# Seeding PSUM from ScalarE, separate steps for the low weight parts, and two more pairs by seven products, in a one-core hybrid attention block

## The chip, the cores and the metric

The kernel runs on one core of a Trainium2 chip. The metric is the device time of one execution in microseconds (us), the median of three runs. The kernel before takes 421.79 us (runs: 422.27, 421.79, 421.65).

The names of the engines: PE is TensorE, which multiplies matrices (PEld: its weight loads), DVE is VectorE, ACT is ScalarE, POOL is GpSimd, SP issues transfers. Matrix products land in PSUM, eight banks of 128 x 512 fp32 each (here `ps0` to `ps7`). Everything else lives in SBUF.

## What is computed

One layer of a streaming encoder: 512 tokens, width 1024. One input projection feeds two attention branches; each result is gated, projected, and both are merged and projected once more.

```python
h = rmsnorm(x, norm_g[l])
(q_lat, c_kv, k_rope, z_a, q_b, k_b, v_b, z_b,
 q_idx, k_idx, w_idx, gate_a, gate_b) = jnp.split(h @ w_in[l], cuts, axis=-1)
...
y_a = mla_attention(q_nope, q_pe, k_nope, k_pe, v_a, pos) * silu(z_a)
# branch b: each query keeps the 128 best keys by an indexer score, logits get a bias by distance
y_b = dsa_attention(q_b, k_b, v_b, q_idx, k_idx, w_idx, rel_bias, pos, topk) * silu(z_b)
merged = sigmoid(gate_a) * (y_a @ w_o_a[l]) + sigmoid(gate_b) * (y_b @ w_o_b[l])
out = rmsnorm(x + merged @ w_out[l], final_g)
```

## The kernel before, in words

**Numbers in two parts.** Every fp32 operand of a large product is split into a high part (rounded by ACT, `act(hi, raw)`) and a low part (`lo = x - hi`, on DVE or POOL, `lo_part`). A product is three matmuls: high x high, high x low, low x high (`mm3`).

**Order.** The program is made by a planner (`Flow`). Each piece of work is a generator ("thread") with a priority; it asks for buffers, waits for conditions, and yields steps. The planner estimates when each step could start, takes the earliest one and emits it to its engine's queue. On the chip each engine works its queue strictly in that order, so PE's order is fixed when the program is built. Numbers at the end of the file (`SEED`, `PSCORE`, `QUEUE`, `SPARE` and others) set priorities, buffer limits and the order of the weight jobs.

**Jobs.** `QUEUE` lists the weight jobs. A lower-case name (`zb1`) is a plain job: `proj` multiplies one 128-column tile of weights with all 512 tokens, 8 x 3 = 24 matmuls of 128x512. Names in upper case come in pairs (`GB0 GB1`): `proj2` makes two tiles from seven half products instead of eight (Winograd's form of Strassen's method), each of 12 matmuls of 128x256. In `seven` the partial sums are put together: ACT copies a finished PSUM bank into an SBUF tile `s_pair`, and DVE adds PSUM banks to it.

**Heads of branch b.** For each of eight heads `dsa_base` adds the reversed bias row and the mask of kept keys on DVE into the tiles `s_p`, ahead of time. `dsa_head` then has PE make the logits of four query tiles (128, 256, 384 and 512 keys wide), two matmuls each, in any bank that is free. DVE adds `s_p` and takes the maximum (line 1946), ACT takes the exponential, PE turns the tiles (identity matmuls, line 477) and multiplies them with the values `vv`.

**End.** `s_ys` (gated attention results) go through 192 matmuls, `s_wo` through the last ones, and `finish` and `scale_out` normalise and store.

**What touches what.** `split_w`, `split_t` and their callers: low parts. `seven`: order of the products and partial sums. `dsa_base`, `dsa_head`: bias and mask. `Pool_.give`: which free bank is taken. `QUEUE`: `zb0` to `zb3`.

Of the kernel before, what the change touches and what calls it, by code (L numbers as in the profile page):

```python
# [16 lines left out]
ALU = mybir.AluOpType  # L17
# [29 lines left out]
class Buf:  # L47


    def __init__(self, tile, name):  # L50
        self.tile, self.name, self.w, self.r, self.written = tile, name, 0.0, 0.0, False
        self.by, self.reads, self.bank = None, {}, False
# [71 lines left out]
class Pool_:  # L124
# [163 lines left out]
SEED = 1  # L288
# [5 lines left out]
def tile_block(ctx: ExitStack, tc: tile.TileContext, a: dict, out: bass.AP, bias_dram: bass.AP):  # L294
# [32 lines left out]
    for b in PS.free:  # L327
        b.bank = True
# [125 lines left out]
    def mm(ps, pairs, start, stop, more=False):  # L454


        def emit():
            for i, (l, r) in enumerate(pairs):
                nc.tensor.matmul(ps.ap, l.ap, r.ap, start=start and i == 0, stop=stop and i == len(pairs) - 1, skip_group_check=more)  # L459
# [12 lines left out]
    def turn(parts):  # L472


        def emit():
            for d, s in parts:
                nc.tensor.transpose(d.ap, s.ap, ident.tile)  # L477
# [94 lines left out]
    def warm_up():  # L572

        ps = yield bank("pv")
        z = zero.tile.bitcast(BF16)
        for _ in range(NWARM):
            yield pe(0.43, [ps.all], [zero.all], lambda: nc.tensor.matmul(  # L577
                ps.tile.rearrange("p (a b) -> p a b", b=P), z, z.rearrange("p (a b) -> p a b", a=1).to_broadcast([P, NT, P]), start=True, stop=True))
        put(ps)
# [103 lines left out]
    def split_w(raw, w, dst, key, cls="w", cap=None, release=False, early=False, added=False, high=None):  # L683
# [6 lines left out]
        if added and not early:  # L690
            yield from lo_added(lo[:, :w], raw, hi[:, :w])
        else:
            step = lo_part(lo[:, :w], raw, hi[:, :w])
            yield soon(step) if early else step
        if release:
            put(raw.buf)
        dst[key] = (hi, lo)
# [209 lines left out]
    def scores(i):  # L907
        n = P * (i + 1)
        work = mask_in_order(i)
        for h in range(NH):  # L910
            yield Until(lambda: h in qs and ks)
            ps = yield bank("lg")
            yield pe(0.005 + n / 2400, [ps.all], [qs[h].all, ks[0].all], lambda: nc.tensor.matmul(  # L913
                ps.tile[:, :n], qs[h].tile[:96, TOK[i]], ks[0].tile[:96, :n], start=True, stop=True))
# [114 lines left out]
    def bias_table():  # L1029
# [16 lines left out]
        for tp, o, c0, c1 in ((toep, oh[0], 0, 320), (toep2, oh[1], 320, 640)):  # L1046
            ps = yield bank("pv")
            yield pe(0.148, [ps.all], [rbs.all, o.all], lambda: nc.tensor.matmul(
                ps.tile[:, :320], rbs.tile, o.tile[:, :320], start=True, stop=True))
# [30 lines left out]
    def splitter():  # L1080
        for job in jobs:
# [7 lines left out]
            for p, w in enumerate(job.widths):  # L1089
                o = sum(job.widths[:p])  # L1090
                yield from split_w(job.raw[:, o : o + w], w, job.parts, p, job.cls, job.cap, p == len(job.widths) - 1, high=job.high, added=w == S and job.src.tensor.name in ADDW and (p > 0 or len(job.widths) == 1))
# [73 lines left out]
    def proj2(first, second):  # L1165
# [7 lines left out]
        def split_t(n, x):  # L1173
# [4 lines left out]
            if n in ADDP:  # L1178
# [1348 lines left out]
```

## Time and profile before

| | |
|---|---|
| runs | 422.27, 421.79, 421.65 us, median 421.79 |
| profiled execution, span from first to last instruction | 420.8 us (the page gives no other time of that execution; 1.0 us under the median) |
| PE | 2414 matmuls in the record |
| last matmul of the program begins and ends in | the piece from 408.47 to 414.27 us |
| end of the last computing instruction | 417.21 us (ACT, from 416.49, 0.72 us) |

The profile is read in this order below: the page's head (busy shares), the waits of PE's weight loads, matmul counts in stretches of time, and then the groups of instructions that the change adds or removes. A matmul's row in the profile has a duration of several hundred ns because it covers the passage through the array; several are in flight at once, so the issue interval, and not that duration, is what a matmul costs.

### The profile page before, as it was taken

To read this page: it belongs to the slowest core of one execution; us is meant where nothing else is said; L and a number is where in the kernel's file an instruction comes from. 1 tells how busy PE (TensorE), PEld (TensorE's weight loads), DVE (VectorE), ACT (ScalarE), POOL (GpSimd) and SP (SyncE) were. 2 spreads that over 40 slices of the span, in tenths; PEclk is the share of its full clock that TensorE was granted. 3 is DMA by queue.
4 is the path that set the end of the run, shared out by engine and by line. 5 is a ranking of instruction groups with operands and counts; after the bars stand their busy time and mean duration, and the time that the engine had idled before them with its cause. 6 is when DMAs were issued, how large, how long until landed. Compare 5 with 4: busy or idle time off the path is not lost.

```text
span 420.8 us, 7354 instructions
## 1 busy us (share of the span) xinstructions
PE 412.9 (98%) x2414; PEld 367.8 (87%) x2414; DVE 387.0 (92%) x845; ACT 273.1 (65%) x612; POOL 98.2 (23%) x122
## 2 busy tenths in 40 slices
PE   9999999999999999999999999999999999999993
PEld 6999988898888888888999998899988888888883
DVE  4869899999999999999889999999999887999984
ACT  5786997476484778647745488496578834346634
POOL 1023766535546434102111010021000100000212
PEclk9999999999999999999999999999999999999997
DMA  8973435906546721351334626441684884738205
GB/s 256 394 286 118 140 106 151 251 26 170 152 99 165 213 72 58 119 138 50 95 107 151 170 95 178 136 125 29 175 275 138 288 291 136 242 104 254 113 2 199
DMA packets 30279, 65.90 MB, mean 157 GB/s; under 512 B 4649, under 2 KB 5689, under 8 KB 30241
## 3 DMA queue, kind: packets, MB, share of 16 engines
q1 hardware_dynamic: 29120, 63.82, 48.8%
q0 software_dynamic: 832, 1.22, 1.2%
q8 instruction: 19, 0.31, 0.3%
q10 hardware_dynamic: 288, 0.39, 0.3%
q14 instruction: 20, 0.16, 0.1%
HBM read 50.49 MB, written 4.21 MB: 130 GB/s over the span
## 4 chain that ended last, share of the span: by engine, by line
PE 84%; DVE 8%; ACT 3%; issue 1%; DMA 1%; POOL 1%; POOLq 0%; DVEq 0%; ACTq 0%
PE ps L459 75%; PE ps L477 4%; DVE s_w L382 2%; DMA raw<-w_o 1%; PE ps L1830 1%; PE ps L1831 1%; PE ps L1829 1%; PE ps L577 1%; PE ps L913 1%; ACT s_p L360 1%; DVE s_p L1946 1%; DVE s_y L382 1%; ACT s_w L351 1%; DVE s_p L382 1%; POOL raw L384 1%
## 5 line engine op out<-in xcount | busy, mean ns | idle before, releaser
L459 PE MATMUL ps<-s_h,s_w 128*128 128x512 f32 (+1 forms) x696 | 152.0, 362 | 0.0
L459 PEld LDWEIGHTS ps<-s_h,s_w 128*128 128x128 f32 x696 | 114.6, 189 | 16.1
L351 ACT CAST s_w<-raw 128x512 fp32r<-128x512 f32 (+3 forms) x130 | 74.6, 594 | 24.0 <-DMA raw<-w_o 8.1
L382 DVE TENSOR_TENSOR s_w<-raw,s_w 128x512 fp32r<-128x512 f32 (+2 forms) x93 | 60.1, 663 | 4.1 <-ACT s_w L351 2.6
L384 POOL TENSOR_TENSOR s_w<-raw,s_w 128x512 fp32r<-128x512 f32 (+2 forms) x37 | 44.2, 1197 | 78.9 <-ACT s_w L351 56.0
L459 PE MATMUL ps<-s_ys,s_w 128*128 128x512 f32 x192 | 44.0, 390 | 0.1
L459 PEld LDWEIGHTS ps<-s_ys,s_w 128*128 128x128 f32 x192 | 36.0, 188 | 7.9 <-DVE s_ys L394 0.4
L459 PE MATMUL ps<-s_hs,s_w 128*128 128x256 f32 x288 | 40.2, 285 | 0.1
L459 PEld LDWEIGHTS ps<-s_hs,s_w 128*128 128x128 f32 x288 | 36.8, 191 | 0.5 <-DVE s_pair L382 0.3
L459 PE MATMUL ps<-s_wo,s_mg 128*128 128x512 f32 (+1 forms) x156 | 33.0, 373 | 0.0
L459 PE MATMUL ps<-s_w,s_xg 128*128 128x328 f32 (+1 forms) x192 | 32.8, 324 | 0.1
L360 ACT ACTIVATE s_p<-s_p,sm 128x512 f32<-128x512 f32 (+3 forms) x56 | 30.5, 563 | 3.3 <-DVE sm L1946 2.4
L459 PEld LDWEIGHTS ps<-s_wo,s_mg 128*128 128x128 f32 x156 | 27.6, 188 | 5.2
L459 PEld LDWEIGHTS ps<-s_w,s_xg 128*128 128x128 f32 x192 | 31.4, 188 | 0.6 <-ACT s_rbc L351 0.5
L939 DVE MATCH_REPLACE8 mask<-sm,mask 128x256 f32<-128x256 f32 (+2 forms) x48 | 25.8, 541 | 0.0
L938 DVE MAX8 sm<-mask 128x8 f32<-128x256 f32 (+2 forms) x48 | 25.1, 547 | 0.1
L360 ACT ACTIVATE s_p<-ps,sm 128x128 f32<-128x128 f32 (+3 forms) x32 | 16.7, 527 | 9.7 <-DVE sm L1814 9.4
L477 PE MATMUL ps<-ident,s_p 128*128 128x128 f32 x160 | 22.8, 273 | 0.0
L459 PE MATMUL ps<-s_lat,s_w 128*128 128x512 f32 x78 | 21.0, 397 | 0.0
L477 PEld LDWEIGHTS ps<-ident,s_p 128*128 128x128 f32 x160 | 18.7, 140 | 2.4
L382 DVE TENSOR_TENSOR s_ph<-ps,s_ph 128x512 fp32r<-128x512 f32 (+1 forms) x32 | 18.5, 614 | 0.6 <-ACT s_ph L351 0.6
L382 DVE TENSOR_TENSOR s_pair<-ps,s_pair 128x256 f32<-128x256 f32 (+1 forms) x35 | 15.9, 455 | 2.0 <-PE ps L459 1.9
(211 smaller groups left out, 767.9 us busy)
## 6 DMA issues: line engine op xcount, KB each, us to landing
raw<-w_out SPq DMA_DIRECT2D x18, 512.0 KB, 4.7
s_op<-s_op SPq DMA_DIRECT2D x36, 128.0 KB, 3.0
raw<-w_ga SPq DMA_DIRECT2D x8, 512.0 KB, 4.2
raw<-w_gb SPq DMA_DIRECT2D x8, 512.0 KB, 3.9
raw<-w_o SPq DMA_DIRECT2D x16, 256.0 KB, 3.3
s_x<-xT SPq DMA_DIRECT2D x8, 256.0 KB, 4.9
s_xn<-x SPq DMA_DIRECT2D x8, 256.0 KB, 6.3
raw<-w_za SPq DMA_DIRECT2D x4, 512.0 KB, 4.8
```

What stands on the lines that cost most here:

```text
L351: nc.scalar.copy(dst.ap, src.ap)
L360: nc.scalar.activation(dst.ap, src.ap, func, **kw)
L382: opts.append(("DVE", 0.07 + 0.00104 * x.n, lambda: nc.vector.tensor_tensor(dst.ap, x.ap, y.ap, op=op)))
L384: opts.append(("POOL", 0.15 + 0.0021 * x.n, lambda: nc.gpsimd.tensor_tensor(dst.ap, x.ap, y.ap, op=op)))
L459: nc.tensor.matmul(ps.ap, l.ap, r.ap, start=start and i == 0, stop=stop and i == len(pairs) - 1, skip_group_check=more)
L477: nc.tensor.transpose(d.ap, s.ap, ident.tile)
L577: yield pe(0.43, [ps.all], [zero.all], lambda: nc.tensor.matmul(ps.tile.rearrange("p (a b) -> p a b", b=P), z, z.rearrange("p (a b) -> p a ...
L913: yield pe(0.005 + n / 2400, [ps.all], [qs[h].all, ks[0].all], lambda: nc.tensor.matmul(ps.tile[:, :n], qs[h].tile[:96, TOK[i]], ks[0].til ...
L938: yield Step([("DVE", t, lambda: nc.vector.max(m8.tile, work.ap))], [m8], [mask[i]])
L939: yield Step([("DVE", t + 0.068, lambda: nc.vector.match_replace(work.ap, m8.tile, work.ap, MARK))], [mask[i]], [m8])
L1829: nc.tensor.matmul(o, q0[0:100], k0[0:100], start=True, stop=False)
L1830: nc.tensor.matmul(o, q0[0:96], k1[0:96], start=False, stop=False)
```

## The change

Five things change together.

1. **PSUM seeded by ACT.** A matmul without `start` adds onto what the bank holds, where an earlier matmul has marked the columns. The planner now keeps those marks (`marked`, `product_to`); an unmarked bank first gets one matmul of zeros (`zeros`). In `seven`, ACT copies product 1 from its bank into a second bank and product 6 is added there, then 7, then 4; DVE adds only twice per pair instead of five times. In `dsa_head`, ACT copies the reversed bias into the bank, the logits are added by PE, and DVE's one pass adds the mask. `dsa_base` shrinks to the load of the bias; its 32 additions go.
2. **Banks are kept apart.** `give` prefers, for logits (`lg`), two banks set aside for them, and for turned tiles (`pt`) two others.
3. **Low parts are own steps** (threads with priority `PLOW`), so that a job's high parts don't wait for its low parts in the plan.
4. **Two more pairs.** `zb0` and `zb1`, `zb2` and `zb3` become `ZB0 ZB1` and `ZB2 ZB3`.
5. **Numbers of the planner**: `SEED`, `PSCORE`, `PSUMS`, buffer limits and `SPARE`.

```diff
+    def zeros(ps, t):
+        z = zero.tile.bitcast(BF16)
+        def emit():
+            product_to(ps.all, True)
+            nc.tensor.matmul(ps.tile.rearrange("p (a b) -> p a b", b=P), z, ..., start=True, stop=True)
+        return pe(t, [ps.all], [zero.all], emit)
...
-        self.free.sort(key=lambda b: max(b.w, b.r))
+        self.free.sort(key=lambda b: (getattr(b, "kept", None) != (req.cls if req.cls in ("lg", "pt") else None), max(b.w, b.r)))
...
         x = yield bank("mm")
         yield from times(1, x)
-        spawn(take("1", act(c22, part(x))), 0)
         y = yield bank("mm")
-        yield from times(6, y)
-        yield Until(lambda: "1" in sums)
-        spawn(take("u2", add(c12, y, c22)), 0)
+        if not marked(part(y)):
+            yield zeros(y, 0.23)
+        spawn(take("seed", act(part(y), part(x))), -1)
+        w = yield bank("mm")
+        yield from times(5, w)
+        yield Until(lambda: "seed" in sums)
+        yield from times(6, y, True)
+        spawn(take("u2", act(c12, part(y))), -1)
         yield from times(2, x, True)
         spawn(take("c11", act(c11, part(x)), x), 0)
         yield Until(lambda: "u2" in sums)
         yield from times(7, y, True)
-        spawn(take("u3", add(c21, y, c22), y), 0)
...
+        spawn(take("u3", act(c21, part(y))), -1)
+        def rest():
+            yield Until(lambda: "u3" in sums)
+            spawn(take("c22", add(c22, w, c21)), -1)
+            yield from times(4, y, True)
+            yield Until(lambda: "c22" in sums)
+            spawn(take("c21", act(c21, part(y)), y), 0)
+            yield from times(3, w, True)
+            spawn(take("c12", add(c12, w, c12), w), 0)
+            pair_done()
+        spawn(rest(), PREST)
...
-            yield mm(ps[:, :nn], [(q, kh[:, :nn]), (q, kl[:, :nn])], True, True)
+            if not marked(ps[:, :nn]):
+                yield zeros(ps, 0.23)
+            yield act(ps[:, :nn], backward(bias.all.f[:, :nn]))
+            yield mm(ps[:, :nn], [(q, kh[:, :nn]), (q, kl[:, :nn])], False, True, True)
...
-QUEUE = '... sb0 zb0 ga6 ga7 VB SB1 GB0 GB1 SB2 zb1 zb2 GB2 GB3 SB3 GB4 GB5 zb3 gb6 ou ou gb7 ou'
+QUEUE = '... sb0 ga6 ga7 VB SB1 GB0 GB1 SB2 ZB0 ZB1 GB2 GB3 SB3 GB4 GB5 ZB2 ZB3 gb6 ou ou gb7 ou'
```

In the built program PE has 96 matmuls `s_h,s_w 128x512` fewer, 72 `s_h,s_w 128x256` and 96 `s_hs,s_w 128x256` more, and one matmul of zeros more. All other kinds of matmul keep their counts. DVE loses 14 additions `s_pair<-ps,s_pair 128x256`, three of 128x512 and 31 `s_p<-s_bias,mask` (POOL had the 32nd). ACT gains 32 copies `ps<-s_bias`, nine copies from bank to bank, 20 `s_pair<-ps 128x256`, two of 128x512, and six casts of weights. POOL makes seven low parts `s_w<-raw` fewer, and DVE 11 more.

The first place is PE's queue at the logits of one head of branch b (`s_op,qhi` are the logits' matmuls, two to a tile; `s_hs,s_w` and `s_h,s_w` are parts of projection jobs). Before, the four tiles went into four banks:

```order
L459 MATMUL ps1_93<-s33_op475_2990,qhi2_74 128x128
L459 MATMUL ps6_98<-s38_op468_2923,qhi2_74 128x256
L459 MATMUL ps6_98<-s33_op475_2990,qhi2_74 128x256
L459 MATMUL ps0_92<-s9_hs348_2175,s40_w485_3078 128x256
L459 MATMUL ps0_92<-s45_hs349_2176,s40_w485_3078 128x256
L459 MATMUL ps7_99<-s38_op468_2923,qhi2_74 128x384
L459 MATMUL ps7_99<-s33_op475_2990,qhi2_74 128x384
L459 MATMUL ps2_94<-s38_op468_2923,qhi2_74 128x512
```

Now, at the same head, the second tile goes into the bank of the first one:

```order
L479 MATMUL ps7_99<-s68_op469_2961,qhi2_74 128x128
L479 MATMUL ps3_95<-s16_hs330_2021,s70_w472_2974 128x256
L479 MATMUL ps3_95<-s52_hs349_2127,s70_w472_2974 128x256
L479 MATMUL ps3_95<-s67_hs359_2223,s70_w472_2974 128x256
L479 MATMUL ps3_95<-s14_hs374_2309,s70_w472_2974 128x256
L479 MATMUL ps2_94<-s30_h112_584,s20_w474_2998 128x256
L479 MATMUL ps2_94<-s65_h113_585,s20_w474_2998 128x256
L479 MATMUL ps2_94<-s66_h114_608,s20_w474_2998 128x256
L479 MATMUL ps2_94<-s69_h115_609,s20_w474_2998 128x256
L479 MATMUL ps2_94<-s71_h117_618,s20_w474_2998 128x256
L479 MATMUL ps2_94<-s72_h118_619,s20_w474_2998 128x256
L479 MATMUL ps7_99<-s38_op459_2886,qhi2_74 128x256
```

Ten projection matmuls now stand between two tiles of one head, and the later tile's bank must be read by DVE and refilled by ACT in that time.

The second place is the work that moved from DVE to ACT. Before, DVE's queue held the bias additions of a head among the additions of a pair's partial sums (`s_pair`) and the low parts (`s_w`):

```order
L382 TENSOR_TENSOR s54_p447_2810<-s32_bias446_2808,mask0_109 128x128
L382 TENSOR_TENSOR s68_p448_2811<-s32_bias446_2808,mask1_110 128x256
L382 TENSOR_TENSOR s54_p447_2810<-s32_bias446_2808,mask2_111 128x384
L382 TENSOR_TENSOR s15_w472_2961<-raw2_68,s19_w471_2960 128x512
L382 TENSOR_TENSOR s24_pair461_2899<-ps2_94,s20_pair462_2900 128x256
L382 TENSOR_TENSOR s21_w474_2982<-raw0_66,s16_w473_2981 128x512
```

Now ACT's queue holds, late in the program, where two heads run at once:

```order
L370 COPY ps7_99<-s1_bias567_3652 128x128
L370 COPY ps6_98<-s1_bias567_3652 128x256
L370 COPY s6_pair608_3909<-ps3_95 128x256
L370 COPY ps7_99<-s1_bias567_3652 128x384
L379 ACTIVATE s20_p619_3990,sm7_83<-s20_p619_3990,sm12_88 128x128
L379 ACTIVATE s68_p621_3992,sm7_83<-s68_p621_3992,sm0_76 128x256
L370 COPY ps6_98<-s1_bias567_3652 128x512
L370 COPY s70_pair606_3907<-ps1_93 128x256
L370 COPY ps7_99<-s53_bias579_3733 128x128
```

The bias copies, the exponentials of an earlier tile and the pair's copies share one queue.

The third place is PE's queue where branch b's last head ends and the products with `s_ys` begin. Before, they followed the last head's products with the values directly:

```order
L459 MATMUL ps0_92<-s5_last6_129,vv0_70 128x256
L459 MATMUL ps0_92<-s4_last5_128,vv0_70 128x128
L459 MATMUL ps0_92<-s5_last6_129,vv0_70 128x128
L459 MATMUL ps6_98<-s47_ys664_4190,s67_w634_4037 128x512
L459 MATMUL ps6_98<-s71_ys668_4194,s67_w634_4037 128x512
```

Now 15 matmuls of a projection stand in between, of which these are the last:

```order
L479 MATMUL ps3_95<-s71_h117_618,s31_w644_4139 128x512
L479 MATMUL ps3_95<-s0_h119_625,s40_w643_4138 128x512
L479 MATMUL ps3_95<-s7_h120_626,s40_w643_4138 128x512
L479 MATMUL ps3_95<-s0_h119_625,s31_w644_4139 128x512
L479 MATMUL ps1_93<-s34_ys669_4287,s14_w650_4178 128x512
L479 MATMUL ps1_93<-s53_ys673_4291,s14_w650_4178 128x512
```

In exchange, the first `s_ys` now belong to a step that comes after the last head in ACT's and DVE's queues; before they came after the last head but one.

More of the change, by code (lines that the diff above doesn't have):

```diff
@@ L326, in tile_block, with spot, marked, product_to @@
     ps_bufs = set(id(b) for b in PS.free)
-    for b in PS.free:
-        b.bank = True
+    for i, b in enumerate(PS.free):
+        b.bank, b.kept, b.marks = True, (None, "pt", "lg")[max(i // 2 - 1, 0)], np.zeros((4, 512), bool)
+    def spot(v):
+        ap, whole = v.ap, v.buf.tile
+        row = whole.ap[0][0]
+        first, col = divmod(ap.offset - whole.offset, row)
+        cols = np.array([col])
+        for step, n in ap.ap[1:]:
+            cols = (cols[:, None] + step * np.arange(n)[None, :]).ravel()
+        return slice(first // 32, (first + ap.ap[0][1] + 31) // 32), cols
+    def marked(v):
+        rows, cols = spot(v)
+        return v.buf.marks[rows, cols].all()
+    def product_to(v, start):
+        rows, cols = spot(v)
+        if start:
+            v.buf.marks[rows] = False
+        v.buf.marks[rows, cols] = True
     def in_ps(v):
@@ L574, in warm_up @@
         ps = yield bank("pv")
+        for _ in range(NWARM):
+            yield zeros(ps, 0.43)
+        put(ps)
+    def zeros(ps, t):
         z = zero.tile.bitcast(BF16)
[L576 to L579, printed above, removed]
+        def emit():
+            product_to(ps.all, True)
+            nc.tensor.matmul(ps.tile.rearrange("p (a b) -> p a b", b=P), z,
+                             z.rearrange("p (a b) -> p a b", a=1).to_broadcast([P, NT, P]), start=True, stop=True)
+        return pe(t, [ps.all], [zero.all], emit)
     def setup_pool():
@@ L689, in split_w, with low @@
             high[key] = hi
[L690 to L692 removed]
+        def low():
             step = lo_part(lo[:, :w], raw, hi[:, :w])
             yield soon(step) if early else step
[L695 to L697 removed]
+            if release:
+                put(raw.buf)
+            dst[key] = (hi, lo)
+        if early:
+            yield from low()
+        else:
+            spawn(low(), PLOW)
     def early_x():
@@ L1177, in split_t, with low @@
             high[n] = hi
-            if n in ADDP:
-                yield from lo_added(lo.all, x, hi.all)
-            else:
+            def low():
                 yield soon(lo_part(lo.all, x, hi.all))
-            parts[n] = (hi, lo)
+                if release:
+                    put(release)
+                made.add(n)
+                parts[n] = (hi, lo)
+            spawn(low(), PLOW)
         def prep(job):
@@ L1293, in hold, with low @@
             yield Until(lambda: True)
+        made = set()
         def split_t(n, x, release=None):
-            r = []
+            r, left = [], []
+            def low(i, hi, lo):
+                yield soon(lo_part(lo.all, x[i], hi.all))
+                left.append(i)
+                if len(left) == 2:
+                    if release:
+                        put(*release)
+                    made.add(n)
+                    parts[n] = r
             for i in range(2):
@@ L1300, in split_t @@
                 yield act(hi.all, x[i])
-                if n in ADDV:
-                    yield from lo_added(lo.all, x[i], hi.all)
-                else:
-                    yield soon(lo_part(lo.all, x[i], hi.all))
                 r.append((hi, lo))
-            if release:
-                put(release)
-            parts[n] = r
+                spawn(low(i, hi, lo), PLOW)
         def prep(job):
```

144 lines of the change are left out of this document (58 added, 86 removed).

## The prediction

> **What bounds the kernel now.** The first view is the page's head: busy shares, granted clock and the chain that ended last.
>
> ```profile
> span 420.8 us, 7354 instructions
> PE 412.9 (98%) x2414; PEld 367.8 (87%) x2414; DVE 387.0 (92%) x845; ACT 273.1 (65%) x612; POOL 98.2 (23%) x122
> PEclk9999999999999999999999999999999999999997
> PE 84%; DVE 8%; ACT 3%; issue 1%; DMA 1%; POOL 1%; POOLq 0%; DVEq 0%; ACTq 0%
> ```
>
> PE is busy for 98% of the span, at full clock. But DVE is at 92%, and PE's busy time counts matmuls that are merely in flight, so the share alone does not show who waits. The second view is therefore the waits of PE's weight loads, which start as soon as an operand is there.
>
> ```profile
> PEld ps L459 <- ACT s_rbc L351: 0.5, 1, 0.5
> PEld ps L459 <- DVE s_ys L394: 0.4, 1, 0.4
> PEld ps L459 <- ACT s_xg L360: 0.3, 1, 0.3
> PEld ps L459 <- DVE s_pair L382: 0.3, 1, 0.3
> PEld ps L459 <- DVE s_last L382: 0.2, 1, 0.2
> ```
>
> That is the whole list behind the warm-up matmuls: five waits, 1.7 us together. So PE's own list of matmuls sets the end; a nearly full DVE stops it almost nowhere. The third view gives what one matmul costs: counts in a stretch and in its second half. The difference is free of the matmuls that straddle an edge.
>
> ```profile
> 172.00:192.00 20.00, 20.00 (x92) 1.00 0.44 126
> 182.00:192.00 10.00, 10.00 (x48) 1.00 0.37 99
> 200.00:220.00 20.00, 20.00 (x169) 1.00 0.34 107
> 210.00:220.00 10.00, 10.00 (x86) 1.00 0.38 127
> 352.00:372.00 20.00, 20.00 (x90) 1.00 0.67 210
> 362.00:372.00 10.00, 10.00 (x46) 1.00 0.68 218
> ```
>
> From 172 to 182 us the queue holds only matmuls of 128x512: 92 - 48 = 44 in 10 us, 227 ns each. From 352 to 362 it is 90 - 46 = 44 again. From 200 to 210 us only 128x256 are at work: 169 - 86 = 83 in 10 us, 120.5 ns each. A half-width matmul thus costs 53% of a full one, and seven of them against four full ones are 0.84 us against 0.91: the gain by sevenths is 7%, not 12.5%.
>
> **The change, part by part.** Two more pairs first, the only part that shortens PE's list. It removes 96 x 227 ns = 21.8 us and adds 168 x 120.5 ns = 20.2 us: **-1.6 us**. The rows of the groups give the other bound:
>
> ```profile
> L459 PE MATMUL ps<-s_h,s_w 128*128 128x512 f32 x480 | 122.2, 397 | 0.0
> L459 PE MATMUL ps<-s_hs,s_w 128*128 128x256 f32 x288 | 40.2, 285 | 0.1
> L459 PE MATMUL ps<-s_h,s_w 128*128 128x256 f32 x216 | 29.9, 284 | 0.0
> L577 PE MATMUL ps<-zero 128*128 128x512 bf16 x10 | 4.4, 631 | 1.0 <-DVE neghalf L532 1.0
> ```
>
> Busy time by count is 255 ns, 140 ns and 138 ns, which gives 24.4 - 23.4 = 1.0 us. It includes the passage through the array at the end of each run, which overlaps the next group, so I take the counts in a stretch.
>
> Here the Trainium skill can be weighed ("TensorE: Matmul & The Clock Gate", Back-to-back issue gap): it gives 518 array cycles at 2.4 GHz for 512 columns and 262 for 256, 216 and 109 ns. By its figures, an estimate, the part would bring 20.7 - 18.3 = 2.4 us. The stretches above show 227 and 120.5 ns, 11 ns more at either width; what is fixed per matmul counts against a change that has 72 matmuls more. Here the measurement decides.
>
> The **matmul of zeros** is one. The warm-up shows ten in 4.4 us, 0.44 each, at the start; the stretches show 0.23 for the same number of columns. It stands in mid-program, so 0.23; bounds 0.23 and 0.44. PE's list is therefore shorter by 21.8 - 20.2 - 0.2 = **1.4 us** (bounds 0.6 from busy time by count with a slow zero matmul, and 1.4).
>
> **Work on DVE and ACT.** These rows price what moves:
>
> ```profile
> L382 DVE TENSOR_TENSOR s_pair<-ps,s_pair 128x256 f32<-128x256 f32 x30 | 12.5, 416 | 0.1
> L382 DVE TENSOR_TENSOR s_p<-s_bias,mask 128x512 f32<-128x512 f32 x8 | 5.5, 682 | 0.0
> L382 DVE TENSOR_TENSOR s_p<-s_bias,mask 128x384 f32<-128x384 f32 x7 | 3.8, 546 | 0.0
> L382 DVE TENSOR_TENSOR s_p<-s_bias,mask 128x256 f32<-128x256 f32 x8 | 3.3, 414 | 0.0
> L382 DVE TENSOR_TENSOR s_w<-raw,s_w 128x512 fp32r<-128x512 f32 x78 | 52.6, 688 | 3.5 <-ACT s_w L351 2.1 <-PE ps L477 1.3
> L360 ACT ACTIVATE ps<-ps 128x512 f32<-128x512 f32 x8 | 4.7, 585 | 1.4 <-PE ps L913 1.3
> L360 ACT ACTIVATE ps<-ps 128x384 f32<-128x384 f32 x8 | 3.7, 467 | 1.7 <-PE ps L913 1.5
> L360 ACT ACTIVATE ps<-ps 128x256 f32<-128x256 f32 x8 | 3.0, 372 | 0.9 <-PE ps L913 0.9
> L351 ACT COPY s_pair<-ps 128x256 f32<-128x256 f32 x12 | 4.4, 364 | 5.2 <-PE ps L459 5.2
> L351 ACT CAST s_w<-raw 128x512 fp32r<-128x512 f32 x106 | 63.5, 620 | 23.1 <-DMA raw<-w_o 8.1 <-DVE raw L382 6.4 <-PE ps L459 4.9
> ```
>
> DVE loses 5.5 + 3.8 + 3.3 us of bias additions (and eight short ones) and 14 x 0.42 = 5.9 us of pair additions, and takes 11 x 0.69 = 7.6 us of low parts, most of them from POOL: over 10 us less in 387. ACT never wrote a bias into PSUM before; the nearest rows read PSUM and write it, 585, 467 and 372 ns, and a cast from SBUF to SBUF takes 620 at 512 columns. At those prices the bias copies are about 8 x (0.6 + 0.47 + 0.37 + 0.3) = 14 us, the pairs' copies 29 x 0.37 = 11, six casts 3.7: ACT goes from 273 to some 302 us, 72% of the span. Neither is on the path while PE has other matmuls to do; both count only where PE waits. That ACT's write to PSUM might take up to the SBUF price would add 1 us to ACT's 302, and nothing to the end.
>
> **New waits.** Before, a logits tile went into any free bank. Now DVE must read the earlier tile, ACT must refill the bank, and only then PE goes on. The links of that chain:
>
> ```profile
> L1946 DVE CUSTOM_DVE_ANT_0 s_p<-ps,s_p 128x128 f32<-128x128 f32 x8 | 2.2, 281 | 1.1 <-PE ps L459 0.9
> L459 PE MATMUL ps<-s_op,qhi 128*128 128x128 f32 x16 | 2.7, 248 | 0.0
> ```
>
> ```profile
> 331.53 0.62 DVE s_ys L394
> 332.14 0.04 issue
> 332.19 1.89 PE ps L459 x7
> ```
>
> The last three, from the chain that ended last, show a hand-over: DVE ends at 332.14, PE starts 0.04 us later. At the place shown in the first program order (128-wide tile, then the 256-wide one in the same bank) the chain is: passage of the last matmul 0.25 - 0.11 = 0.14, DVE 0.28, ACT 0.37, three hand-overs 0.12, together 0.9 us. Ten matmuls of 120.5 ns, 1.2 us, lie between. It fits with 0.3 us to spare if both queues are free at that moment. One 512-wide low part ahead on DVE (0.69) would make PE wait 0.4 us. Of the 32 tiles eight open a head and find their bank long free; 24 depend. Behind a waiting bias copy stand, in ACT's queue, exponentials and copies of the pair, which the transposes and the next product wait for.
>
> In the pairs the seed copy (0.36 us) is covered by product 5, 12 matmuls or 1.4 us, since product 6 comes after it; the copy of the sum in that bank is covered by product 2, again 1.4 us, and then product 7 follows. Before, the same bank waited for a DVE addition (0.42) behind the same product 2. These nine copies I cost at nothing; without their cover each would cost about 0.6 us.
>
> For all new waits together I take **0 to +0.5 us**, nearer to zero: the order before was laid by the same planner, with DVE at 92%, and it waits five times in all. Bounds: 0, and 24 x 0.4 = 9.6 us if every tile that depends comes late.
>
> **Waits that go.** The three waits of the list that lie behind the first 50 us sum to 0.9 us. The wait for `s_ys` (0.4) has 15 matmuls of 227 ns, 3.4 us, put ahead of it, but its work now stands behind the last head: copy to `s_tmp`, addition, then cast and low part of `s_ys`, each 0.6 to 0.7 us, some 2.6 us with hand-overs, plus whatever ACT has queued ahead. It may go or stay. The others may come back elsewhere. So 0 to -0.9, and I take -0.2, which cancels against the new waits. The start does not move: the first 290 rows of PE's order are the same. The end is the same sequence too:
>
> ```profile
> 407.98 1.38 DVE s_xr L394 x2
> ...
> 414.75 1.12 issue
> 415.87 0.59 POOLq L2523
> 416.49 0.72 ACT s_rg L360
> ```
>
> Low parts as own steps and the planner's numbers have no price of their own: they change the order, and show only as waits. SP issues one transfer more, two halves of `w_o` in place of one piece.
>
> **Sum.** 420.8 - 1.4 = 419.4 us of span. The median of the runs is 421.79, 1.0 us above the span; that part (start and end of the program) stays, so **420.4 us**, 0.33% less. A measurement of this kernel can tell about 0.2%, 0.84 us, from no change.
>
> **The rivals.** *More waits than before, gain eaten.* The chain over two kept banks, DVE to ACT to PE, comes late at some tiles. For it: the spare time is 0.3 us and DVE was almost always busy; four banks became two. Against it: DVE is relieved of over 10 us, and ACT was idle a third of the time. Two or three tiles late by 0.4 us give 421.4. *Slower.* The same chain, at the four places where two heads run at once: there one head's bias copies stand in ACT's queue ahead of the other's, each behind DVE's read, so a late read delays both heads and the projections' copies behind them. It decides from 2.2 us of waits on (1.4 gained plus 0.84), that is from six of 24 tiles late by a whole low part; ten of them, 4 us, give 424.4, six give 422.8. *Waits close as well.* DVE's relief removes most of the 0.9 us: 419.6. *The 256-wide matmuls gain nothing.* With the rows' busy time by count the list shrinks by 0.6 to 0.8 us: 421.1. The counts in the stretches speak against it. *No fixed cost per matmul.* The stretches give 227 - 120.5 = 106.5 ns for 256 columns, so 14 ns of each matmul do not depend on its width. If the new pairs escaped that, their 72 additional matmuls would cost 1.0 us less, and the time would be 419.4. Nothing in the stretches speaks for it. The figures of the Trainium skill cited above point that way.
>
> **How the numbers follow.** Forecast, 419.9 to 420.9: 0.53. Waits close as well, below 419.9: 0.15. No fixed cost per matmul: 0.02. Gain eaten, or the half-width matmuls gain little, 420.9 to 422.6: 0.18. Slower, above 422.6: 0.12. Predicted time **420.4 us**. The range leaves out the upper 0.12 and some 0.05 below 419.3: **419.3 to 422.6**. Faster by over 0.2% (below 420.95) is 0.70, slower (above 422.63) 0.12, the rest 0.18.
>
> **What would show it.** PE in the new profile has 2487 or so matmuls, and a stretch of 128x256 still counts 83 in 10 us. The list of PEld's waits should stay under some 2 us in all. If the forecast fails upward, that list names `ACT ps` (a bias or seed copy) as releaser, at PE rows of `s_op,qhi`; if it names `DVE s_w`, the low parts as own steps are late instead. DVE's busy time should fall to about 375 us, ACT's rise to about 300. Wrong would be: many short waits on ACT, or an `s_ys` wait longer than the 0.4 us of before.

## The result, and the profile after

| kernel | median us (range, runs) | ratio to before, 95% interval |
|---|---|---|
| before | 422.03 (421.65 to 422.42, 4) | |
| changed | 424.88 (424.48 to 425.56, 4) | 1.0072 [1.0058, 1.0087] |

The changed kernel is 2.9 us slower. Predicted was 420.4 us, 0.33% faster, with a range that ended at 422.6: the direction was wrong. The profiled execution has a span of 423.8 us, against 420.8; it took 425.56 us, the longest of the four. Medians, ranges and ratios in this document leave out three disturbed executions, one of e3 (436.82 us) and two of e13 (beyond 1,400 us).

First the page's head of the changed kernel (busy time, share, instructions; then the shares of the chain that ended last).

```profile
span 423.8 us, 7541 instructions
PE 413.6 (98%) x2487; PEld 368.8 (87%) x2487; DVE 378.7 (89%) x804; ACT 297.5 (70%) x682; POOL 100.9 (24%) x127
PE 65%; DVE 20%; ACT 5%; issue 4%; DMA 2%; POOL 1%; SPq 1%; POOLq 0%; DVEq 0%; ACTq 0%
```

Matmuls and ACT came out as worked out (2487 and about 300 us); DVE fell by 8.3 us, where over 10 were expected. But the chain that ended last runs through PE for only 65%, where it was 84%, and through DVE for 20%, where it was 8%. The next view says where: the waits of PE's weight loads (us in total, times, longest), without those of the warm-up.

```profile
PEld ps L479 <- ACT s_wo L370: 1.3, 1, 1.3
PEld ps L1894 <- ACT s_p L379: 1.1, 1, 1.1
...
PEld ps L498 <- DVE s_lat L413: 1.0, 1, 1.0
PEld ps L479 <- DVE s_wo L401: 0.6, 1, 0.6
PEld ps L479 <- ACT ps L370: 0.6, 3, 0.2
PEld ps L498 <- DVE s_ph L401: 0.5, 2, 0.3
PEld ps L479 <- ACT s_xg L379: 0.5, 1, 0.5
PEld ps L479 <- ACT s_rbc L370: 0.5, 1, 0.5
PEld ps L946 <- DVE mask L413: 0.4, 1, 0.4
PEld ps L479 <- ACT s_w L370: 0.2, 1, 0.2
PEld ps L479 <- DVE s_w L401: 0.2, 1, 0.2
```

These are 6.9 us, against 1.7 before. For the matmuls themselves the view of PE's waits names four:

```profile
PE ps L479 <- ACT s_wo L370: 0.9, 1, 0.9
PE ps L1894 <- ACT s_p L379: 0.6, 1, 0.6
PE ps L498 <- DVE s_lat L413: 0.5, 1, 0.5
PE ps L479 <- DVE s_wo L401: 0.3, 1, 0.3
```

Before, it names none behind the warm-up. The four stand at 409 us (`s_wo`, the operands of the output's last products), 138 us (`s_p`, a logits tile of the first eight heads) and 53 us (`s_lat`). The wait for `s_lat` is not the same in every execution: in the eight runs below that keep the changed kernel's order up to there (e1, e5, e7, e9, e10, e16, e17, e18) the weight loads wait 0.5 us for it, not 1.0, and 0.2 to 1.0 us for `s_p`. The counts in a stretch of full-width matmuls are the ones of before (stretch; busy us and instructions of PE, PEld, DVE, ACT, POOL; clock, DMA share, GB/s):

```profile
352.00:372.00 20.00, 20.00 (x90) 16.49 (x89) 18.07 (x32) 7.69 (x13) 0.74 (x1) 1.00 0.56 189
362.00:372.00 10.00, 10.00 (x46) 8.20 (x45) 9.97 (x19) 3.36 (x6) 0.74 (x1) 1.00 0.68 215
```

Of 128x512 there are again 90 - 46 = 44 in 10 us. From 200 to 210 us 166 - 84 = 82 are counted where 83 were, but 14 of them are now turns of `s_p`, 128x128, so this count says little of the half-width ones. The matmuls' starts in the trace say more: from one to the next it is 227 ns in the median behind a 128x512 of `s_ys,s_w` and 120 ns behind a 128x256 of `s_hs,s_w`, in both kernels. So PE's list is shorter as worked out, and the loss is in waits.

### The profile page after: what moved, and what is told of

Its sections match the earlier page's. It is cut to its first block, busy times and chain, and to the rows that moved or that the text cites. A ratio compares the mean times of both kernels' runs of the same rounds, so it can differ in the third digit from the quotient of the medians.

```text
span 423.8 us, 7541 instructions
## 1 busy us (share of the span) xinstructions
PE 413.6 (98%) x2487; PEld 368.8 (87%) x2487; DVE 378.7 (89%) x804; ACT 297.5 (70%) x682; POOL 100.9 (24%) x127
## 4 chain that ended last, share of the span: by engine, by line
PE 65%; DVE 20%; ACT 5%; issue 4%; DMA 2%; POOL 1%; SPq 1%; POOLq 0%; DVEq 0%; ACTq 0%
PE ps L479 57%; PE ps L498 4%; DVE s_wo L401 2%; DVE s_mg L401 2%; ACT s_w L370 2%; DVE s_w L401 1%; DVE s_wsum L401 1%; DMA raw<-w_out 1%; DVE s_rg L401 1%; DVE s_x L413 1%; DVE mask L972 1%; DVE s_pair L401 1%; PE ps L606 1%; PE ps L946 1%; DVE s_xr L413 1%
## 5 line engine op out<-in xcount | busy, mean ns | idle before, releaser
L479 PE MATMUL ps<-s_h,s_w 128*128 128x512 f32 (+1 forms) x672 | 139.2, 350 | 0.0
L479 PEld LDWEIGHTS ps<-s_h,s_w 128*128 128x128 f32 x672 | 106.6, 189 | 13.4 <-ACT s_w L370 0.2
L370 ACT CAST s_w<-raw 128x512 fp32r<-128x512 f32 (+3 forms) x134 | 77.4, 596 | 18.5 <-DVE raw L401 9.3
L401 DVE TENSOR_TENSOR s_w<-raw,s_w 128x512 fp32r<-128x512 f32 (+2 forms) x104 | 67.1, 663 | 6.9 <-ACT s_w L370 6.2
L479 PE MATMUL ps<-s_hs,s_w 128*128 128x256 f32 x384 | 53.5, 285 | 0.0
L403 POOL TENSOR_TENSOR s_w<-raw,s_w 128x512 fp32r<-128x512 f32 (+2 forms) x30 | 35.0, 1173 | 77.6 <-DVE s_ys L413 36.9
L479 PEld LDWEIGHTS ps<-s_hs,s_w 128*128 128x128 f32 x384 | 49.2, 191 | 0.4
L379 ACT ACTIVATE s_p<-s_p,sm 128x512 f32<-128x512 f32 (+3 forms) x58 | 31.6, 564 | 0.1
L370 ACT COPY s_tmp<-ps 64x512 f32<-64x512 f32 (+1 forms) x18 | 10.1, 562 | 15.5 <-PE ps L479 8.7
L1977 DVE CUSTOM_DVE_ANT_0 s_p<-ps,mask 128x128 f32<-128x128 f32 (+3 forms) x32 | 15.3, 486 | 4.9 <-PE ps L479 4.7
```

The source lines that it names most:

```text
L370: nc.scalar.copy(dst.ap, src.ap)
L379: nc.scalar.activation(dst.ap, src.ap, func, **kw)
L401: opts.append(("DVE", 0.07 + 0.00104 * x.n, lambda: nc.vector.tensor_tensor(dst.ap, x.ap, y.ap, op=op)))
L403: opts.append(("POOL", 0.15 + 0.0021 * x.n, lambda: nc.gpsimd.tensor_tensor(dst.ap, x.ap, y.ap, op=op)))
L1977: step = Step([("DVE", 0.1 + 0.00104 * n, lambda: nc.vector.tensor_tensor_reduce(p.ap, ps.tile[:, :n], mask[i].tile, op0=ALU.add, op1=ALU. ...
```

## The experiments

The theories, by the letters that the expectations use. **A, A2**: waits at a few places of the new order, the largest at the end. **B, E**: the hand-over from ACT to PE on banks that ACT fills, all along the heads. **C**: the half-width pairs gain nothing. **D, F**: DVE and ACT have no room, so a wait that is removed comes back. **G**: any fresh set of the planner's numbers does as well.

| run | median us (range) | ratio to before, 95% interval |
|---|---|---|
| e1_no_reserve | 424.84 (424.02 to 425.15) | 1.0067 [1.0055, 1.0079] |
| e2_pairs_only | 427.91 (427.75 to 428.76) | 1.0146 [1.0133, 1.0159] |
| e3_no_pairs | 431.66 (429.76 to 434.94) | 1.0236 [1.0204, 1.0268] |
| e4_old_numbers | 432.18 (431.25 to 433.19) | 1.0233 [1.0219, 1.0246] |
| e5_reserve_4 | 424.23 (423.71 to 424.73) | 1.0054 [1.0041, 1.0068] |
| e6_free_mla_banks | 424.60 (423.94 to 425.14) | 1.0063 [1.0050, 1.0076] |
| e7_bias_twice | 436.14 (435.50 to 436.91) | 1.0338 [1.0324, 1.0352] |
| e8_new_numbers | 426.65 (425.17 to 427.62) | 1.0110 [1.0090, 1.0129] |
| e9_bias_half | 423.95 (422.01 to 425.00) | 1.0047 [1.0031, 1.0062] |
| e10_reserve_2 | 424.29 (423.76 to 424.59) | 1.0054 [1.0042, 1.0066] |
| e11_best_guess | 423.93 (423.33 to 425.16) | 1.0053 [1.0038, 1.0067] |
| e12_low_inline | 435.40 (435.08 to 435.71) | 1.0318 [1.0305, 1.0331] |
| e13_chain_told_15 | 422.59 (421.89 to 426.61) | 1.0028 [1.0009, 1.0047] |
| e14_chain_told_25 | 427.01 (426.32 to 428.04) | 1.0123 [1.0107, 1.0139] |
| e15_numbers_only | 424.82 (424.14 to 425.98) | 1.0075 [1.0061, 1.0090] |
| e16_seeds_quarter | 423.43 (423.21 to 423.66) | 1.0039 [1.0027, 1.0051] |
| e17_end_relieved | 423.37 (422.90 to 423.99) | 1.0037 [1.0024, 1.0050] |
| e18_both | 423.93 (423.04 to 425.29) | 1.0051 [1.0038, 1.0065] |

### The parts one by one

```diff
-SPARE = {'w': 2, 'wo': 6, 'sig': 3}
+SPARE = {'w': 2, 'sig': 3}
```

> The changed kernel with one number taken back: no six buffers of the class wo held in reserve. PE's order is the same for its first 2080 rows; only the last loads move (three of the last four w_out loads go ahead of those of x again). Theory A (the loss is waits that the new order of jobs leaves at a few places, the largest at the end): the two waits of PE's weight loads for s_wo (1.3 and 0.6 us) go, 424.9 - 1.7 = 423.2 us, ratio to before about 1.003. Theory B (the seeds and biases that ACT writes into the banks delay PE all along the heads): the end changes little that matters, 424.5 to 424.9. Theory C (the half-width pairs gain nothing): as B.

424.84 us, no gain. The waits for `s_wo` are gone; in the list of weight-load waits stand two others in their place:

```profile
PEld ps L479 <- ACT s_ys L379: 1.1, 1, 1.1
...
PEld ps L479 <- DVE s_ys L413: 0.8, 1, 0.8
```

1.9 us, as much as went. Without a reserve the w_out weights are split earlier, ahead of the work that `s_ys` needs; with it, too late for the last products. Theory A missed this. The time is what B and C had forecast, but the list of waits shows the exchange, which is neither's mechanism.

```diff
-QUEUE = '... sb0 zb0 ga6 ga7 VB SB1 GB0 GB1 SB2 zb1 zb2 GB2 ... GB5 zb3 gb6 ...'
+QUEUE = '... sb0 ga6 ga7 VB SB1 GB0 GB1 SB2 ZB0 ZB1 GB2 ... GB5 ZB2 ZB3 gb6 ...'
```

> The kernel before with only the new list of jobs: the two more pairs by seven products, but sums, biases and low parts as before and no zero matmul. Theories A and B: PE's list shrinks by 96 x 227 ns and grows by 168 x 120.5 ns, -1.6 us: 420.4 us if the waits stay near 1.7 us, more by what waits come in. Theory C: 422.0, no change, with the same waits. DVE gets 14 more additions of 0.42 us, so up to 1 us of new waits would not surprise.

427.91 us, 5.9 slower than before and beyond what any theory had. The list of waits and two stretches of this run:

```profile
PEld ps L459 <- ACT s_w L351: 3.9, 4, 1.6
PEld ps L459 <- DVE s_w L382: 2.8, 4, 1.3
```

```profile
240.00:260.00 20.00, 19.12 (x152) 18.53 (x151) 19.76 (x51) 15.49 (x39) 3.62 (x3) 1.00 0.45 122
260.00:280.00 20.00, 18.33 (x148) 17.76 (x148) 19.93 (x47) 11.83 (x27) 1.53 (x2) 1.00 0.39 125
```

DVE is busy for 19.76 and 19.93 of 20 us, and PE, at 19.12 and 18.33, waits for weights. A full DVE alone does not explain that: in the same stretches of the kernel before it has 19.96 and 19.35, and PE its 20.00. In the changed kernel, where the other parts relieve it, DVE has 16.61 and 18.03, and PE 20.00. That fits pairs that need this relief; it does not show it, since the order differs too.

The reverse, the changed kernel with the old QUEUE line, and the changed kernel with all of the planner's old numbers (PHCAP, TCAP, PSCORE, YSB, PSUMS, PCAP, SUMS_AT, SPARE):

> The changed kernel with the old list of jobs: biases and seeds in the banks and low parts as own steps, without the two more pairs. PE's order is that of the changed kernel for the first 1014 rows. Theory A: the list is 1.6 us longer, the waits of the first 195 us (latraw 0.7, bank of the mla logits 0.8) stay, the end may come out either way: 424.8 to 426.5. Theory B: with half the seeds less is lost: about 424. Theory C: the list is as long as that of the changed kernel, 424.9.

> The changed kernel with all of the planner's numbers of before (caps, priorities, reserves, places of the sums). Seeds, biases, low parts and pairs stay. Theory A: the waits fall at other places, the end has its w_out loads partly ahead of x: 422 to 424.5, and which places wait is another list. Theory B: what ACT's seeds cost stays, about 424.9. Theory C: 424.9 or a little less.

431.66 and 432.18 us: above all that was expected. Both have other orders; e3 waits longest for `s_ys` (1.5 us), e4 for `s_ph`, `s_p`, `s_xr` and `s_w`. Likewise the kernel before with the new numbers, all its work unchanged:

> The kernel before with the planner's numbers of the changed kernel, nothing else; no work is added or taken away, so PE's list is as long as before. If the numbers are fitted to one list of jobs (as the changed kernel with the old numbers, 432 us, suggests), this costs several us of waits: 424 to 432. If the new numbers are simply better or have no price, 421 to 422.5.

426.65 us, 4.7 more than before, as the first of the two forecasts had it: the numbers fit one list of jobs. And the low parts back in their place:

```diff
-            spawn(low(), PLOW)
+            yield from low()
```

> The changed kernel with the low weight parts issued in their place again instead of as own steps. PE's order up to row 297 is that of the kernel before, not of the changed one. If own steps have no price and no worth (as the prediction had it), the wait for s_lat at 53 us goes and the rest stays: 424.2 us. If they are what keeps DVE's and ACT's queues from blocking each other: 426 or more, with waits for s_w. If they are what the changed kernel loses by: 423 or less.

435.4 us, 10.5 above the changed kernel, as the second of the three forecasts had it:

```profile
PEld ps L479 <- ACT s_w L370: 4.0, 8, 1.0
PEld ps L479 <- ACT s_ys L379: 2.5, 1, 2.5
PEld ps L479 <- ACT s_pair L370: 2.3, 4, 1.0
...
PEld ps L498 <- DVE s_lat L413: 0.2, 1, 0.2
```

As own steps they are worth much, at least with these numbers, which were fitted with them. The wait for `s_lat` is 0.2 us, where the runs with own steps have 0.5 (the profiled changed kernel 1.0), so most of it comes with the own steps.

### The waits, one place at a time

```diff
-SPARE = {'w': 2, 'wo': 6, 'sig': 3}
+SPARE = {'w': 2, 'wo': 4, 'sig': 3}
```

> The changed kernel with a reserve of four buffers of wo in place of six. PE's whole order is the same; SP's differs only in its last loads, and ACT, DVE and POOL split the last w_out weights earlier. Theory A2 (the reserve of six is what makes the last products wait, since their operands need buffers of that class; four are enough to keep them away from the s_ys stretch): neither wait, for s_wo (1.9 us) or s_ys (1.9 us in the run without a reserve), is there: 423.2 us, ratio 1.003. Rival D (ACT and DVE have no time left from 300 us on, so that a wait that is removed comes back elsewhere in full, as it did without the reserve): 424.8.

```diff
-            ps = yield bank("lg")    # in mla_head
+            ps = yield bank("lm")
```

> As the run with a reserve of four, and the logits of the first eight heads (two matmul passes more each, no bias) go into any free bank again; the two kept banks serve the biased heads alone. PE's last 1208 rows are the same as in the changed kernel. Theory A2: the wait of 1.1 us at 138 us (PE 0.8) goes too, the early ones for s_lat (0.7) may move: 422.2 to 422.6. Rival D: 424.0 to 424.8.

> The changed kernel with a reserve of two. PE's order is that of the changed kernel up to row 2292, so past the products with s_ys; two of the last w_out loads go ahead of those of x. Theory A2: no wait for s_wo and none for s_ys, and the last weights are split earlier, so that DVE's last additions are not held up as with a reserve of four (there the end behind the last matmul was 7.5 us in place of 6.7): 423.2 us. Rival D: 424.2 to 424.8, the end long or a wait elsewhere.

> Reserve of two and free banks for the logits of the first eight heads, together. Theory A2: what the two bring adds up, 422.8 to 423.2. Rival D: 424.2 and more; the wait at 138 us is gone, others of the same sum stand at 200 to 226 us.

424.23, 424.60, 424.29 and 423.93 us. Reserve of four: the waits for `s_wo` and `s_ys` are both out of the list, 1.9 us, but only 0.65 us is won. Free banks: the wait for `s_p` is gone, and the same view names other ones, among them `s_pair` (0.7 us) and an `s_p` of DVE (0.5). Reserve of two: no `s_wo` and no `s_ys`, but `s_mg` (0.8) and `s_w` (0.7).

A2's times came out in none of the four. D's did for e6 and e10; e5 and e11 lie between the two. The four medians are 0.7 us apart, with ranges of 0.8 to 1.8 us each, so they do not rank these variants: a removed wait mostly comes back, and at most a part is won.

### The hand-over and the end, with all orders frozen

In five runs only the length or the number of some copies or additions changes, and no engine's order does (but for the reserve of four in the last).

```diff
-            yield act(ps[:, :nn], backward(bias.all.f[:, :nn]))
+            seed = act(ps[:, :nn], backward(bias.all.f[:, :nn]))
+            eng, t, emit = seed.options[0]
+            seed.options = [(eng, t, lambda: (emit(), emit())[1])]
+            yield seed
```

> The changed kernel with each of the 32 bias copies from ACT into a bank issued twice in a row, all orders as they are; ACT works 14 us more, and each biased tile comes 0.27 to 0.58 us later, the last link before its matmul. Theory A2 (the chain DVE, ACT, PE has slack at nearly all tiles): at most 1 us more, 424.9 to 425.9. Theory B (the chain is late all along the heads): the 24 tiles that depend on a bank just read lose about 0.4 us each, up to 9 us more: 429 to 434.

> The changed kernel with each bias copy from ACT cut to the first half of its columns (the biases of the other half are left out), all orders as they are. ACT works some 5 us less and each biased tile is ready 0.1 to 0.3 us earlier. If the chain over the two kept banks is what the changed kernel loses by now (theory B), all of its waits for a bank filled by ACT go, with the short gaps of 0.1 us behind them, 1.5 us or more: 423.4 or less. If it just fits (A2: 0.6 us of waits in the list, and doubling it costs 11 us because there is no slack, not because it is late now): 424.2 to 424.6.

Doubled: 436.14 us, 11.3 more, beyond even what theory B had:

```profile
PEld ps L479 <- ACT ps L370: 11.2, 20, 1.4
```

Twenty waits of 0.56 us on average, all at matmuls of `s_op,qhi`: nearly every biased tile that depends is late when ACT needs one more copy. Halved: 423.95 us, 0.9 less, with executions from 422.01 to 425.00 us, between what the two theories gave. So the chain has no slack, and as it stands is only a little late.

```diff
+    def short(dst, src):
+        step = act(dst, src)
+        (eng, t, _), n = step.options[0], src.n // 4
+        step.options = [(eng, t, lambda: nc.scalar.copy(dst[:, :n].ap, src[:, :n].ap))]
+        return step
-            yield act(ps[:, :nn], backward(bias.all.f[:, :nn]))
+            yield short(ps[:, :nn], backward(bias.all.f[:, :nn]))
-        spawn(take("seed", act(part(y), part(x))), -1)
+        spawn(take("seed", short(part(y), part(x))), -1)
```

> The changed kernel with every copy that ACT makes into a bank ahead of a product cut to the first quarter of its columns: the 32 bias copies and the eight seeds of the pairs (three quarters of the biases and seeds are left out). All orders as they are. If the hand-over ACT to PE is the main price of the change (theory E): the loss of 2.9 us shrinks by 1.5 us or more, 423.4 or less. If it is a small one beside the waits at the end, at 53 and 138 us (A2): about 1 us, as with the biases cut to half, 423.8 to 424.3.

```diff
-                yield soon(tt(r, r, u, ALU.add, BOTH))
+                step = soon(tt(r, r, u, ALU.add, BOTH))
+                step.options = [... the same on r[:, :128], u[:, :128] ...]
+                yield step
```

> The changed kernel with the six additions of partial sums onto x near the end cut to the first quarter of their columns (three quarters are left out), all orders as they are; DVE works some 2.5 us less between 402 and 406 us. If the wait for s_wo at 409 us comes from DVE's full queue there (rival D): the waits for s_wo shrink by most of their 1.9 us, 423.0 to 423.4. If it comes from the buffers of wo alone, given back late: 424.5 to 424.9.

> Reserve of four, and the copies into the banks cut to a quarter (three quarters of biases and seeds are left out). If the hand-over and the end are the two main terms, they add up: 424.2 less what the copies bring in the first of these runs, 422.3 to 423.2, and what is left above the time before minus 1.4 us is the waits for s_lat, s_p and the long end. If one hides the other: 423.8 and more.

Copies cut: 423.43 us, **1.45 less**. No `ACT ps` is left in the list (0.6 us); the waits for `s_wo` shrink too, from 1.9 to 1.1 us. That is theory E's price, at its edge. End relieved: 423.37 us, **1.5 less**, as rival D had it, and `s_wo` is out of the list. The stretch of 402 to 412 us in before, changed and e17:

```profile
402.00:412.00 10.00, 10.00 (x51) 8.40 (x51) 8.20 (x18) 3.50 (x11) 2.22 (x3) 1.00 0.01 2
```

```profile
402.00:412.00 10.00, 8.84 (x44) 6.97 (x43) 10.00 (x19) 2.94 (x9) 1.29 (x1) 1.00 0.00 1
```

```profile
402.00:412.00 10.00, 10.00 (x51) 8.41 (x51) 8.89 (x22) 4.23 (x12) 1.31 (x1) 1.00 0.00 2
```

DVE is busy for 8.20, 10.00 and 8.89 of 10 us; PE gets 51, 44 and 51 matmuls through. What fills DVE shows in its timeline (start, us, operation, idle before), first before, then changed:

```profile
399.73 3.69 DVE L382 TENSOR_TENSOR s_xr<-s_xr,s_part 128x512 f32<-128x512 f32 x6
...
406.00 0.68 DVE L382 TENSOR_TENSOR s_wo<-raw,s_wo 128x512 fp32r<-128x512 f32 x1
407.98 1.38 DVE L394 SCALAR_TENSOR_TENSOR s_xr<-ps,s_xr 128x512 f32<-128x512 f32 x2 [1.30 <-PE ps L459]
```

```profile
402.46 3.69 DVE L401 TENSOR_TENSOR s_xr<-s_xr,s_part 128x512 f32<-128x512 f32 x6
...
408.66 0.68 DVE L401 TENSOR_TENSOR s_wo<-raw,s_wo 128x512 fp32r<-128x512 f32 x1
409.26 0.67 DVE L401 TENSOR_TENSOR s_wo<-s_wsum,s_wo 128x512 fp32r<-128x512 f32 x1
409.87 1.28 DVE L401 TENSOR_TENSOR s_wo<-raw,s_wo 128x512 fp32r<-128x512 f32 x2
```

Before, one low part of w_out lies behind the six additions, and DVE then waits for PE. In the changed kernel DVE begins the additions 2.7 us later, four low parts lie behind them, and PE waits for DVE. The longer of PE's two waits there names ACT, but ACT is held up by DVE too: its last two casts of w_out stand behind work on `s_xr` that waits for DVE. (Before, ACT's last cast of w_out began at 397.75 us, ahead of that work.)

```profile
406.84 0.63 ACT L379 ACTIVATE junk<-s_xr 128x512 f32<-128x512 f32 x1 [6.58 <-DVE s_xr L413]
...
408.55 0.60 ACT L370 CAST s_wo<-s_wsum 128x512 fp32r<-128x512 f32 x1
409.06 0.62 ACT L370 CAST s_wo<-raw 128x512 fp32r<-128x512 f32 x1
```

The chain that ended last says who sets the end. Before and changed, where it comes to DVE's two additions of a finished bank to x:

```profile
399.99 7.97 PE ps L459 x42
407.96 0.02 issue
407.98 1.38 DVE s_xr L394 x2
```

```profile
408.73 2.41 DVE s_wo L401 x4
411.14 1.20 DVE s_xr L413 x2
```

Before, the chain comes from PE. In the changed kernel it runs up to these additions through DVE from 354.6 us on, behind the arrival of a piece of w_out, with one cast on ACT (398.60 us) and no matmul. The two additions start at 407.98 and, by the timeline, 411.07 us, 3.1 us apart, and the program ends 12.8 and 12.7 us later: the whole difference of the spans is there. With the end relieved (e17) they start at 408.93, the chain comes from PE again, and the end is 12.8 us later. With the reserve of four (e5) they start at 409.86 and the chain still runs through DVE; so 1.9 us of removed waits of PE bring little. Why that piece of w_out arrives only at 354.6 us, no run tests.

Copies cut and reserve of four (e18, which takes the reserve of four for the end, not the short additions): 423.93 us, no better than the copies cut alone, as the second of the two forecasts had it. The timeline of PE's and ACT's last work in this run:

```profile
409.63 4.40 PE L485 MATMUL ps<-s_wo,qhi 128*128 128x512 f32 x30
```

```profile
417.47 0.72 ACT L379 ACTIVATE s_rg<-s_rg,sm 128x512 f32<-128x512 f32 x1 [0.38 <-POOL sm L459]
```

PE ends at 409.63 + 4.40 = 414.03, where the changed kernel's PE ends at 417.05 and that of before at 414.27: the two suspects give PE back 3.0 us in these executions. But the last scaling starts 3.4 us behind PE, where before it started 2.2 behind (416.49). DVE starts the two additions at 409.05 us, 1.1 us later than before, and sets the end in PE's place. That is where the two do not add up.

### Orders laid with the hand-over in mind

```diff
-                b.w = max(b.w, end)
+                b.w = max(b.w, end + (SEEDLAT if eng == "ACT" and b.bank else 0.0))
+SEEDLAT = 0.15
```

in e13 and e14 with the free banks of e6, and with the numbers fitted again (for e13 TCAP 5, PSCORE 10, YSB 5, PLOW 10, PSUMS 9, SUMS_AT ('a', 4), SPARE w 1 and sig 4, BIAS 0.012, YIELD 0.1, SWITCH 0.05).

> The changed kernel, with the planner counting 0.15 us more between an ACT write into a bank and the matmul that adds onto it, its numbers fitted again under that count, and free banks for the logits of the first eight heads. Biases, seeds, low steps and pairs stay. Theory E (the price is the hand-over ACT to PE on the biased tiles, which the order of the changed kernel leaves without slack): the waits on ACT's banks go with their short gaps, 1 to 3 us less than the changed kernel: 421.5 to 423.9. Rival F (DVE and ACT simply have too little room, whatever the order): 424 and more.

> The same with 0.25 us. Theory E: more slack yet at each biased tile, no ACT bank in the list of waits; 420.5 to 423.5, and if below 421.1 then better than the kernel before by more than the measurement leaves open. Rival F: 424 and more.

> The changed kernel with its numbers fitted again in the same way, but with nothing added to the count of the hand-over. Theory E: an order that looks as good on paper has the waits on ACT's banks on the chip, as the changed kernel has: 423.5 to 426. Theory G (any fresh fit of the numbers does as well, the hand-over has nothing to do with it): as the two other runs, 421 to 423.5.

422.59, 427.01 and 424.82 us. No ACT bank is in the list of any of the three, of e15 neither, though its planner counted nothing more. Theory E's time came out for e13, and for e15 without the waits that it named; for e14 it failed: those waits can go without a gain. e13 waits for other things, for `s_pair` (1.6 us in four waits) and `s_xg` (0.7). It is the best order found for the changed work, 2.3 us below the changed kernel. By the medians it is 0.6 us above before; the ratio, 0.28% [0.09%, 0.47%], is carried by three of its ten executions, above 423.7 us. No run beats the kernel before. Neither E nor G holds: three fits of the numbers lie 4.4 us apart. What the hand-over count itself is worth stays open, since e13 and e15 also differ in the banks of the first eight heads and in the numbers.

## Why the prediction was wrong

**Bound of the kernel before, and PE's list: right.** PE's list is 1.4 us shorter: PE has the 2487 matmuls, and with each priced at the median spacing of its kind in the trace of before, the two lists differ by 1.4 us. By the figures that the Trainium skill states for an isolated matmul ("TensorE: Matmul & The Clock Gate", Back-to-back issue gap), 216 and 109 ns, an estimate, a stretch would hold 46 and 92 matmuls in 10 us; the kernel before shows 44 and 83. The rival without a fixed cost per matmul fell, as did theory C: a half-width matmul takes 120 ns in the changed kernel too.

**DVE's and ACT's work: nearly right.** 378.7 and 297.5 us, where about 375 and 300 were worked out; the rows of before priced it.

**"For all new waits together I take 0 to +0.5 us": mis-sized.** The chain was described rightly, and its 0.3 us of spare time too: doubling one link makes 20 tiles late. As it stands it costs up to 1.45 us (e16). The list names 0.6 of it; by the matmuls' starts in the two profiled executions, 0.9 us of PE's gaps go between 180 and 320 us, where the biased heads are, and 0.8 us behind 400 us, at `s_wo`. The sign that the prediction gave, `ACT ps` at rows of `s_op,qhi`, appeared, but three times and 0.2 us at most: the chain is one term, not the answer.

**"The end is the same sequence too": the step that failed most.** The same instructions stand there, but I looked at DVE's last additions alone and not at what is queued ahead of them. That PE's list sets the end held for the kernel before and was carried over. In the changed kernel the chain runs through DVE from 354.6 us on. The reserve of six buffers, which was counted at nothing, lets the last w_out weights be split late; four low parts come behind the additions where one did, DVE is full from 402 to 412 us, and 1.5 us is lost (e17). The wait for `s_ys`, left open, went by the same reserve (e1 has it back, 1.9 us).

**"The start does not move": too short a look.** I compared PE's order alone, and it differs from row 293 on. Just behind it eight transposes of `s_latraw`, which ran at 52.2 us before, start at 53.4 us: more matmuls stand ahead of them, and in the profiled execution PE idles 0.5 us, until DVE has made an `s_lat` from a bank.

**Two kept banks:** only the biased heads were considered. The first eight heads ask for the same class of bank; one of their tiles waits at 138 us for its bank, 0.6 us of PE's time in the profiled execution and at most 0.5 in the runs with the same order there, and does not with free banks (e6).

**"Low parts as own steps and the planner's numbers have no price of their own": wrong by far more than the whole effect.** The numbers shift the time by 4.7 (e8) and 7.3 us (e4), the own steps by 10.5 (e12).

The difference of the two profiled executions can be split by place. A gap is here the time from one matmul's start to the next, less the median of that kind in the trace of before:

| place | changed against before, us |
|---|---|
| PE's list | -1.4 |
| gaps in the first 20 us (between -0.9 and +0.1 in the nine traces with this order) | -0.9 |
| at 40 to 60 us, `s_lat` (+0.4 in the other eight) | +0.8 |
| at 60 to 120 us and 140 to 180 us | +0.4 |
| at 120 to 140 us, `s_p` (0 to +0.8 in the other eight) | +0.9 |
| at 180 to 320 us, the biased heads (copies cut to a quarter: +0.8) | +1.6 |
| at 320 to 340 us, `s_ys` gone | -0.4 |
| behind 400 us, `s_wo` | +1.7 |
| behind the last matmul | +0.2 |

Together that is +2.9, against 3.0 measured. No run isolates a cause for the +0.8 that the heads keep with the copies cut, nor for the +0.4 at 60 to 180 us. The prediction had +0 to +0.5 for all of these gaps and -0.2 for those that go. What stays open is whether any order of the changed work gets below before: none that was run did, and e18 says that an order must also clear DVE's end, not PE's waits alone.

Of the rivals, the one on the slower side named the bias chain as its mechanism and 422.8 to 424.4 us as its price; its size came near, but by luck in part: its mechanism gave at most 1.45 us (e16) of the 4.3 us between the measured time and 422.0 - 1.4 = 420.6 us.

## What to carry to other kernels

Where a planner lays the order, a part that looks free (a reserve, a step of its own, a cap) is a new order for all engines: compare every engine's rows from the first difference on, and ask in each stretch who is full there. A shorter list on the engine that sets the end is worth only what the next engine can follow; here DVE set the pace from 354.6 us to the end. Experiments that keep every order and change only the length of one kind of instruction separate a cost from a new draw of the order; here they sized two costs, where changed orders mostly drew new waits.

## What was not expected of the hardware

A wait of PE costs more than PE's own list says: the next weight load does not start while PE waits. The timeline of the changed kernel behind the wait at 138 us, for PE and its weight loads:

```profile
137.84 0.19 PEld L1894 LDWEIGHTS ps<-s_op,qhi 100*128 100x128 f32 x1 [1.06 <-ACT s_p L379]
137.85 0.45 PE L1894 MATMUL ps<-s_op,qhi 100*128 100x384 f32 x1 [0.62 <-ACT s_p L379]
137.95 0.19 PEld L1895 LDWEIGHTS ps<-s_op,qhi 96*128 96x128 f32 x1
...
138.13 0.34 PE L1895 MATMUL ps<-s_op,qhi 96*128 96x384 f32 x1
138.13 0.19 PEld L1896 LDWEIGHTS ps<-s_op,s_op 96*128 96x128 f32 x1
...
138.31 0.34 PE L1896 MATMUL ps<-s_op,s_op 96*128 96x384 f32 x1
```

The first matmul behind the wait is followed after 0.28 us, the next after 0.18, at the same width: the second weight load began only at 137.95, and its 0.19 us were not covered. By the matmuls' starts in the trace, the one after the first is late by the same 0.11 us behind the waits that end at 271.82 and 409.99 us. The list of weight loads is no exact price either. For the wait at 138 us it gives 1.06 us, PE's own list 0.62; PE lost 0.79 + 0.11 = 0.90 us by the matmuls' starts. For the short one at 271.82 us the weight load waited 0.17 us, PE's list names nothing, and PE lost 0.13 + 0.11 = 0.23 us. So short waits are dearer than they look, and the longest ones cheaper than the weight loads' list says.
